# One transposition of the recurrence a slot later in another PSUM bank, and the attention statistics transposed as a whole tile, a slot later

## The chip, the cores and the metric

The kernel runs on one core of one Trainium2 chip. The metric is the device time of one execution in microseconds; "before" and "after" are compared by the median of several runs. A profile of one execution (a hardware trace) says which engine did what at which time.

The engines named here: TensorE (PE) multiplies matrices, and its weight loads are listed apart as PEld. VectorE (DVE) and ScalarE (ACT) do elementwise work, GpSimd (POOL) a little of it, and SyncE (SP) issues nearly all DMAs. Each engine carries out its own instructions in their order, and waits on semaphores for the others. SBUF is the on-chip memory of 128 partitions; PSUM is the memory that TensorE writes into, in banks of 128 x 512 float32.

## The reference

A trunk of two post-norm layers on x of 1024 positions by 1024 features, all in float32. Layer 0 mixes tokens by dilated attention, layer 1 by a gated linear recurrence (HGRN2). A squared-ReLU MLP with 4096 hidden features follows each.

```python
for i in range(DEPTH):                       # DEPTH = 2
    if i % 2 == 0: y = dilated_attention_mixer(x, attn_w_in, attn_w_out)
    else:          y = hgrn2_mixer(x, hgrn_w_in, hgrn_w_out, hgrn_norm_g, lbs[i])
    x = layer_norm(ALPHA * x + y)
    y = squared_relu_mlp(x, w_up, w_down)
    x = layer_norm(ALPHA * x + y)
```

Attention has three head groups (window 128, 512, 2048; dilation 1, 4, 16) with 16 heads of 64 features each. In every group a query looks at itself and 128 keys behind it in its residue class. The groups are mixed by a softmax over their log-sum-exps:

```python
m = max(s, -1); p = exp(s - m); l = sum(p, -1)
o = (p / l) @ v;  lse = m + log(l)
out = sum_g softmax_g(lse)[g] * o[g]
```

So m and l (the "statistics" below) of all three groups must come together before the outputs are mixed. The recurrence works in chunks of 64 positions, with 8 heads of 128 features; its output is normalised per head and goes through an output projection:

```python
a = where(causal, q_dec @ k_dec.T, 0);  o = a @ v + q_dec @ state
o = o * rsqrt(mean(o*o, -1) + RMS_EPS) * norm_g      # per head
y = o @ w_out
```

## The kernel before

**Stages.** Attention (0 to about 975 us of the span), its output projection with LayerNorm (to 1135), MLP 0 (to 1745), the recurrence (to 2105), its output projection (to 2230), MLP 1 (to the end). Each float32 product is made of three products of high and low parts; in the attention's and the MLPs' projections the 2 x 2 blocks are multiplied by a Strassen-like scheme of seven.

**Attention.** A unit is a pair of heads in one group: 8 pairs x 3 groups (in the order g = 2, 1, 0) = 24 units, and two consecutive ones form a step group gi. One step group has 21 products, each of 12 matmuls; `product(n)` is slot n. Behind each product the program issues the small work that a table put into that slot. For a step group the tables count from `base`, the slot 21 behind the group's first product: its units are worked off while the next group's products run. `OFFS` places six pieces of each unit (`qk`, `vtrans`, `ptr`, `pv`: scores, and the transpositions of v and of the probabilities, and the product with v), `ROPES` the rotary embedding, `STATS` the three steps of `combine_tr`, `MIX` the mixing of the groups (`combine`, `combine_mul`). Unit a=0 of the group has its pieces in slots 4, 6, 8, 10, 12 and 14, unit a=1 in 13, 15, 17, 19, 21 and 23. Within a slot, what was placed by an earlier group comes first, then unit 0's pieces and statistics, then unit 1's. The `in_order` block keeps TensorE and VectorE to the order of the program throughout this loop.

For each query block `qk` takes the (negated) maximum on VectorE (L511) and the exponentials with their sum on ScalarE (L514), and both leave one column in the unit's tile `stats`, 128 x 32: m and l, two heads, eight blocks. `combine_tr` then does three steps: it transposes that tile on TensorE (`mpt`, L564) into a bank of the tag `pt` and copies it out on ScalarE (`sr`, L566); writes it to DRAM (`mdram`, L569); and reads it back rearranged into `ml` (L575, L578). PSUM tags have fixed numbers of banks: `mm` 3, `s` 2, `pt` 2, `o` 1. All transpositions, and the broadcast `fb` of the mixing weights, take `pt`.

After the last step group, what is left of the tables (`done`) and the work of the last two units (`mine`) is put together in 22 lists, which the output projection works off between its own matmuls. There the order on TensorE is not written out. List 9 has unit b's `qk(4)`, list 10 unit a's last `ptr` and all three steps of its `combine_tr`, list 11 unit b's `qk(6)`.

**Recurrence.** For each of 8 heads there are six projections of 24 matmuls (L171 to L173), one per slot, and behind each the program issues one list of the head before: `trans` of v, both `amat`, `trans` of the keys; `kv(0)`; `omat(0)` and `kv(1)`; `omat(1)`; an empty list; `otr(0)` and `otr(1)`. `omat(j)` leaves half j normalised in `on` (VectorE, L1563), `otr(j)` transposes it in four pieces on TensorE (`opt`, L1571, into a `pt` bank), and ScalarE scales it into `oN` (L1572). For heads 0 to 4 the result goes to DRAM. Head 0 has one empty list in front. The lists of consecutive heads are merged index by index, so what a head has beyond six lists falls into the next head's first. The last head's lists are worked off by the output projection, evenly over its 56 steps of three matmuls.

Of the kernel before, what the change touches and what calls it, by code (L numbers as in the profile page):

```python
# [9 lines left out]
F32 = mybir.dt.float32  # L10
F32R = mybir.dt.float32r
U8 = mybir.dt.uint8
AF = mybir.ActivationFunctionType
# [3 lines left out]
P = 128  # L17
# [35 lines left out]
RESIDENT = 2  # L53
MIX = ((20, 21, 21, 24, 25, 30, 31, 32, 33, 33, 34, 35, 35, 36),
       (30, 31, 33, 34, 35, 37, 38, 39, 41, 41, 42, 42, 42, 43))
STATS = ((12, 13, 15), (21, 22, 24))
ROPES = ((-5, -3, -3, -1, 1, 2), (5, 7, 7, 9, 11, 11))
ROPES0 = ((-5, -2, -1, 2), (-4, 0, 1, 4))
OFFS = ((1, 3, 5, 7, 9, 11), (10, 12, 14, 16, 18, 20))
# [3 lines left out]
def trunk_kernel(  # L63
# [24 lines left out]
    nc = tc.nc  # L88
    cp = ctx.enter_context(tc.tile_pool(name="cp", bufs=1))
# [6 lines left out]
    def U(name, dt=F32):  # L96
        return up.tile([P, 1024], dt, name=name, tag="u")

    def bank(tag, name):
        return ps.tile([P, 512], F32, name=name, tag=tag, bufs={"mm": 3, "s": 2, "pt": 2, "o": 1}[tag])  # L100

    def small(shape, name, bufs=4, dt=F32):
        return sp.tile(shape, dt, name=name, tag=name, bufs=bufs)

    act = nc.scalar.activation
# [21 lines left out]
    ident = cp.tile([P, P], F32, name="ident")  # L127
# [194 lines left out]
    def attention(pre, hc):  # L322
# [120 lines left out]
        sel = cp.tile([P, NG * P], F32R, name="bsel")  # L443
        frow = U("frow", F32R)
        mdram = dp.tile([NPAIR, NG, 2, 2, S], F32, name="mdram")

        def constants():
            nc.sync.dma_start(cosT, cos_t)
            nc.sync.dma_start(sinT, sin_t)
            nc.sync.dma_start(mask, masks)  # L450
# [15 lines left out]
        def rope(e, g, nm):  # L466
            rot = U("rot")
            for b4 in range(4):
                o = (b4 ^ 1) * 32
                nc.sync.dma_start(rot[b4 * 32:b4 * 32 + 32, :], e[o:o + 32, :])  # L470
            qT = U(nm)
            nc.vector.tensor_mul(cls(qT, g), nat(e, g), nat(cosT, g))
            return qT, (lambda: nc.vector.tensor_mul(rot, rot, sinT),
                        lambda: nc.vector.tensor_add(cls(qT, g), cls(qT, g), nat(rot, g)))
# [84 lines left out]
                [lambda: pv(6), lambda: pv(7)],  # L559
            ]  # L560

        def combine_tr(pr, g, sS, ml):
            pt = bank("pt", "mpt")
            nc.tensor.transpose(pt[:32, 0:P], sS.rearrange("p w a b -> p (w a b)"), ident)  # L564
            sr = small([32, P], "sr", 2)
            act(sr, pt[:32, 0:P], AF.Copy)  # L566
            yield
            md = mdram[pr, g]
            nc.sync.dma_start(md.rearrange("w h (b q) -> (w h b) q", q=P), sr)  # L569
            yield  # L570

            d = DIL[g]
            for w in range(2):
                if d == 1:
                    nc.sync.dma_start(ml[:, w, 0, :], md[w].rearrange("h (i n) -> (h i) n", n=P))  # L575
                else:
                    for h in range(2):
                        nc.sync.dma_start(  # L578
                            ml[8 * h:8 * h + 8, w, g, :].rearrange("i (r n) -> i r n", r=d),
                            md[w, h].rearrange("(r i n) -> i r n", r=d, i=8))  # L580
            yield

        def combine(pr, ml):
            def cv(tl, g):
                d = DIL[g]
                return tl if d == 1 else tl.rearrange("p (r n) -> p n r", r=d)

            m = ml[:, 0]
            l = ml[:, 1]
            v = nc.vector  # L590
            mn = small([16, P], "mn", 1)
            v.tensor_tensor(nat(mn, 1), nat(m[:, 0], 1), cv(m[:, 1], 1), op=ALU.min)
            v.tensor_tensor(nat(mn, 2), nat(mn, 2), cv(m[:, 2], 2), op=ALU.min)
            for g in range(NG):
                v.tensor_sub(cv(m[:, g], g), nat(mn, g), cv(m[:, g], g))
            act(m, m, AF.Exp)
            yield
            v.tensor_mul(l, l, m)
            den = mn
            v.tensor_add(nat(den, 1), nat(l[:, 0], 1), cv(l[:, 1], 1))  # L600
            v.tensor_add(nat(den, 2), nat(den, 2), cv(l[:, 2], 2))
            yield
            v.reciprocal(den, den)
            for g in range(NG):
                v.tensor_mul(nat(l[:, g], g), cv(m[:, g], g), nat(den, g))

            fh = wp.tile([P, 512], F32R, name="fh", tag="p")[:16, :NG * P].rearrange("p (g t) -> p g t", t=P)
            fl = wp.tile([P, 512], F32R, name="fl", tag="pts")[:16, :NG * P].rearrange("p (g t) -> p g t", t=P)
            act(fh, l, AF.Copy)
            yield  # L610
            v.tensor_sub(fl, l, fh.bitcast(F32))
            yield
            for g in range(NG):
                for i, f in enumerate((fh, fl)):
                    r = 4 * g + 2 * i
                    nc.sync.dma_start(frow[r:r + 2, :].bitcast(F32).rearrange("h (i t) -> h i t", t=P),
                                      f[:, g, :].bitcast(F32))
            yield

        def combine_mul(pr, og, hb):  # L620

            c = slice(hb * 512, hb * 512 + 512)
            acc = og[0]
            for g in GORD:
                fb = bank("pt", "fb")
                nc.tensor.matmul(fb, sel[:, g * P:(g + 1) * P], frow[:, c], start=True, stop=True)
                nc.vector.tensor_mul(og[g][:, c], og[g][:, c], fb)
                yield
            nc.vector.tensor_add(og[2][:, c], og[2][:, c], og[1][:, c])
            nc.vector.tensor_add(acc[:, c], acc[:, c], og[2][:, c])  # L630
            yield
            if hb:
                if pr < SPILL[0]:
                    nc.sync.dma_start(ond[0, pr], acc)
                    oN.append(ond[0, pr])
                else:
                    oN.append(acc)
            yield
# [4 lines left out]
        def at(slot, f):  # L643
            fill.setdefault(slot, []).append(f)

        ep, acc, part = {}, {}, {}
        ml, ogs = {}, {}
# [58 lines left out]
        def unit_work(gi, a, base):  # L706

            pr, g = groups[gi][a]
            if pr not in ml:
                ml[pr] = small([16, 2, NG, P], "ml", 1)  # L710
                ogs[pr] = [None] * NG
            sS = small([P, 2, 2, 8], "stats", 3)

            adds = {}

            def rope_of(t):
                res[a, t], adds[t] = rope(ep.pop((gi, a, 0 if t == 1 else 1)), g, "qT" if t == 0 else "kT")

            def begin():
                ogs[pr][g] = U("og")  # L720
                p = pieces(pr, g, res.pop((a, 0)), res.pop((a, 1)), ep.pop((gi, 2, a)), ogs[pr][g], sS)
                for f in p[0]:
                    f()
                work.extend(p[1:])

            work = []
            later = [lambda: [f() for f in work.pop(0)] for _ in range(5)]
            trs = combine_tr(pr, g, sS, ml[pr])
            stats = [lambda: next(trs, None)] * 3
            mix = []  # L730
            if g == GORD[-1]:
                steps = combine(pr, ml[pr])
                mix = [lambda: next(steps, None)] * 5
                for hb in range(2):
                    muls = combine_mul(pr, ogs[pr], hb)
                    mix += [lambda muls=muls: next(muls, None)] * (4 + hb)
            return adds, rope_of, [begin] + later, stats, mix
# [23 lines left out]
        for n in range(len(seq)):  # L761
            gi, i, j = seq[n]
# [26 lines left out]
            if n % 21 == 14:  # L789
# [3 lines left out]
                for a in range(2):  # L793
                    adds, rope_of, core, stats, mix = work[a]
# [9 lines left out]
                    for k, f in enumerate(core):  # L804
                        at(base + UNIT0 + OFFS[a][k], f)
                    for k, f in zip(STATS[a], stats):
                        at(base + k, f)
# [677 lines left out]
    def hgrn(xs, late, consts, pre, gw):  # L1485
# [8 lines left out]
        def head_pieces(hd, kd, kd2, qd, vT, dec, oNt):  # L1494
# [71 lines left out]

            def otr(j):
                on = st.pop(("on", j))
                pt = bank("pt", "opt")
                for i in range(4):  # L1570
                    nc.tensor.transpose(pt[:, i * P:(i + 1) * P], on[:, i * P:(i + 1) * P], ident)  # L1571
                act(oNt[:, j * 512:(j + 1) * 512], pt, AF.Identity, scale=gT[:, hd:hd + 1])  # L1572
                if hd < SPILL[1] and j == 1:
                    nc.sync.dma_start(ond[1, hd], oNt)
# [4 lines left out]
                [lambda: omat(0), lambda: kv(1)],  # L1579
                [lambda: omat(1)],  # L1580
                [],
                [lambda: otr(0), lambda: otr(1)],
            ]

        oN = []
# [3 lines left out]
        for hd in range(8):  # L1589
# [8 lines left out]
            for t, h in slots:  # L1598
# [7 lines left out]
                o = proj(loaded[bi], xs[h])  # L1606
# [8 lines left out]
                if both and t == 1:  # L1615
# [14 lines left out]
                    b = a1  # L1630
# [9 lines left out]
                if both and t == 0:  # L1640
                    q = e[0]
# [27 lines left out]
    pr = Out(w_attn_out, "a", 0)  # L1669
# [7 lines left out]
    pr = Out(w_hgrn_out, "h", 1)  # L1677
# [81 lines left out]
```

## Time and profile before

| | us |
|---|---|
| median of 3 runs | 2845.02 (2842.76 to 2846.17) |
| profiled execution | 2844.54 |
| its span | 2842.8 |
| TensorE busy | 2772.0 (98%) |
| TensorE weight loads | 2229.9 (78%) |
| VectorE busy | 2068.6 (73%) |
| ScalarE busy | 1449.2 (51%) |
| GpSimd busy | 122.7 (4%) |

The span goes from the first to the last instruction of the trace, and the execution's own time has 1.7 us around it. A row of a timeline gives start, length, engine, line, operation, what it writes <- reads, shape and count, and in brackets the engine's idle time before it with what ended it. In shapes such as 128*32 stand the rows and columns of TensorE's array that a matmul uses. Consecutive like instructions are merged into one row; its length is then from the first start to the last end. Ends of matmuls are modelled, and a matmul's end lies behind the start of the next one in an undisturbed stream. A row of waits gives who waited for whom, us in total, times and the longest. A row of windows gives the stretch and its length, the busy time and number of instructions of PE, PEld, DVE, ACT and POOL, and then the granted clock of TensorE, the mean busy share of the DMA engines, and GB/s. Engine names with a q (SPq) are the sequencers that issue DMAs.

### The profile page before, as it was taken

To read this page: it belongs to the slowest core of one execution; us is meant where nothing else is said; L and a number is where in the kernel's file an instruction comes from. 1 tells how busy PE (TensorE), PEld (TensorE's weight loads), DVE (VectorE), ACT (ScalarE), POOL (GpSimd) and SP (SyncE) were. 2 spreads that over 40 slices of the span, in tenths; PEclk is the share of its full clock that TensorE was granted. 3 is DMA by queue.
4 is the path that set the end of the run, shared out by engine and by line. 5 is a ranking of instruction groups with operands and counts; after the bars stand their busy time and mean duration, and the time that the engine had idled before them with its cause. 6 is when DMAs were issued, how large, how long until landed. Compare 5 with 4: busy or idle time off the path is not lost. (4 is left out here: it accounts for less than half of the span.)

```text
span 2842.8 us, 40144 instructions
## 1 busy us (share of the span) xinstructions
PE 2772.0 (98%) x14280; PEld 2229.9 (78%) x14280; DVE 2068.6 (73%) x3830; ACT 1449.2 (51%) x3105; POOL 122.7 (4%) x67
## 2 busy tenths in 40 slices
PE   8999999999999989999999999999999999999998
PEld 6777777777777767888878887787787788878887
DVE  7768777777777767786686876565667787678677
ACT  5555555555555555544454434555553545454433
POOL 0000000000000003100000011111102200000000
PEclk9999999999999999999999999999999999999999
DMA  7766665766667523464494752101132455475654
GB/s 288 252 200 195 185 206 172 216 198 206 193 194 219 166 87 133 145 226 156 158 320 126 263 177 90 38 31 60 55 117 81 149 204 174 159 271 189 222 175 132
DMA packets 204936, 485.27 MB, mean 171 GB/s; under 512 B 29376, under 2 KB 43712, under 8 KB 204736
## 3 DMA queue, kind: packets, MB, share of 16 engines
q1 hardware_dynamic: 204736, 482.72, 51.5%
q8 instruction: 112, 1.84, 0.3%
q14 instruction: 88, 0.72, 0.1%
HBM read 362.82 MB, written 94.24 MB: 161 GB/s over the span
## 5 line engine op out<-in xcount | busy, mean ns | idle before, releaser
L666 PE MATMUL pmm<-xh,H 128*128 128x512 f32 x1008 | 407.6, 404 | 13.0 <-ACT H L432 8.9
L668 PE MATMUL pmm<-xh,H 128*128 128x512 f32 x1008 | 395.7, 393 | 0.1
L667 PE MATMUL pmm<-xl,H 128*128 128x512 f32 x1008 | 395.6, 392 | 0.0
L666 PEld LDWEIGHTS pmm<-xh,H 128*128 128x128 f32 x1008 | 190.9, 189 | 53.3 <-ACT H L432 8.9
L668 PEld LDWEIGHTS pmm<-xh,H 128*128 128x128 f32 x1008 | 190.2, 189 | 42.3 <-DVE H L440 0.8
L667 PEld LDWEIGHTS pmm<-xl,H 128*128 128x128 f32 x1008 | 191.0, 189 | 36.6
L514 ACT ACTIVATE p<-p,stats 128x128 f32<-128x128 f32 (+1 forms) x384 | 168.3, 441 | 93.6 <-DVE stats L511 92.2
L1260 PE MATMUL pdy<-dT,dS 128*128 128x512 f32 x512 | 199.2, 389 | 0.0
L1263 PE MATMUL pdy<-dT,dS 128*128 128x512 f32 x512 | 199.2, 389 | 0.0
L1264 PE MATMUL pdy<-dT,dS 128*128 128x512 f32 x512 | 199.2, 389 | 0.0
L511 DVE CUSTOM_DVE_ANT_0 p<-s,mask 128x128 f32<-128x128 f32 (+1 forms) x384 | 113.3, 348 | 67.7 <-PE s L500 58.4
L137 ACT ACTIVATE dS<-dr 128x512 fp32r<-128x512 f32 x192 | 119.5, 622 | 73.2 <-PE pdy L1264 36.6
L171 PE MATMUL pmm<-f0nh,wh 128*128 128x512 f32 x384 | 153.2, 399 | 0.0
L173 PE MATMUL pmm<-f0nh,wl 128*128 128x512 f32 x384 | 149.9, 390 | 1.6 <-DVE wl L138 1.6
L172 PE MATMUL pmm<-f0nl,wh 128*128 128x512 f32 x384 | 149.7, 390 | 0.0
L138 DVE TENSOR_TENSOR dS<-dr,dS 128x512 fp32r<-128x512 f32 x192 | 136.2, 710 | 15.8 <-ACT dS L137 13.9
L214 POOL TENSOR_TENSOR z<-z,bB 128x1024 f32<-128x1024 f32 x24 | 58.5, 2442 | 1680.8 <-ACT z L213 1676.7
L527 ACT ACTIVATE pts<-ppt 128x256 f32<-128x256 f32 (+1 forms) x192 | 85.4, 474 | 62.0 <-PE ppt L524 59.8
L137 ACT ACTIVATE dT<-hold 128x512 fp32r<-128x512 f32 x128 | 80.0, 625 | 69.9 <-DVE hold L1239 28.8
L1073 ACT ACTIVATE H<-wc 128x512 fp32r<-128x512 f32 x128 | 77.2, 625 | 73.5 <-DVE wc L1066 44.0
L1263 PEld LDWEIGHTS pdy<-dT,dS 128*128 128x128 f32 x512 | 96.1, 188 | 20.1
L1260 PEld LDWEIGHTS pdy<-dT,dS 128*128 128x128 f32 x512 | 96.1, 188 | 19.8
(395 smaller groups left out, 6950.3 us busy)
## 6 DMA issues: line engine op xcount, KB each, us to landing
xh<-xtd SPq DMA_DIRECT2D x110, 512.0 KB
xl<-xtd SPq DMA_DIRECT2D x110, 512.0 KB
dr<-hd SPq DMA_DIRECT2D x192, 256.0 KB
dr<-in_w_down_dram SPq DMA_DIRECT2D x128, 256.0 KB
rot<-e SPq DMA_DIRECT2D x192, 128.0 KB
wa<-in_w_up_dram SPq DMA_DIRECT2D x48, 512.0 KB
wb<-in_w_attn_dram SPq DMA_DIRECT2D x36, 512.0 KB
wa<-in_w_attn_dram SPq DMA_DIRECT2D x33, 512.0 KB
```

The source lines that it names most:

```text
L137: act(hi, raw, AF.Copy)
L138: nc.vector.tensor_sub(lo, raw, hi.bitcast(F32))
L171: nc.tensor.matmul(o, wh[:, k], xs.h(k), start=k == 0, stop=False)
L172: nc.tensor.matmul(o, wh[:, k], xs.l(k), start=False, stop=False)
L173: nc.tensor.matmul(o, wl[:, k], xs.h(k), start=False, stop=k == NK - 1)
L514: act(p[:, h, :n], p[:, h, :n], AF.Exp, bias=sS[:, 0, h, b:b + 1], scale=-1.0, accum_out=sS[:, 1, h, b:b + 1])
L666: nc.tensor.matmul(o, wh, hi[k // 2][:, c], start=begin and k == 0, stop=False, skip_group_check=True)
L667: nc.tensor.matmul(o, wh, lo[k // 2][:, c], start=False, stop=False, skip_group_check=True)
L668: nc.tensor.matmul(o, wl, hi[k // 2][:, c], start=False, stop=end and k == 3, skip_group_check=True)
L1260: nc.tensor.matmul(o[q], h, T_[:, L], start=begin, stop=False, skip_group_check=True)
L1263: nc.tensor.matmul(o[q], h, T_[:, R], start=False, stop=False, skip_group_check=True)
L1264: nc.tensor.matmul(o[q], l, T_[:, L], start=False, stop=end, skip_group_check=True)
```

## The change

In the recurrence `otr(1)` gets a list of its own behind `otr(0)`'s, a slot later, and its transpositions go into the one `o` bank instead of a `pt` bank. A head has seven lists then, and `otr(1)` falls into the first list of the head after, ahead of that head's `trans`. In the output projection the last head's lists are spread as seven over the same 56 steps.

In attention the `stats` tiles of the units become four slices of 32 columns of one tile `allS` of 128 x 128, zeroed once; unit number 2 gi + a takes slice (2 gi + a) mod 4. `combine_tr` transposes the whole tile and copies and stores only its own 32 rows. All three of its steps are placed one slot later.

```diff
-STATS = ((12, 13, 15), (21, 22, 24))
+STATS = ((13, 14, 16), (22, 23, 25))
...
+        allS = cp.tile([P, P], F32, name="stats")
+        nc.gpsimd.memset(allS, 0.0)
...
-        def combine_tr(pr, g, sS, ml):
+        def combine_tr(pr, g, slot, ml):
             pt = bank("pt", "mpt")
-            nc.tensor.transpose(pt[:32, 0:P], sS.rearrange("p w a b -> p (w a b)"), ident)
-            sr = small([32, P], "sr", 2)
-            act(sr, pt[:32, 0:P], AF.Copy)
+            nc.tensor.transpose(pt[:, 0:P], allS, ident)
+            q = slice(slot * 32, slot * 32 + 32)
+            sr = small([P, P], "sr", 2)
+            act(sr[q], pt[q, 0:P], AF.Copy)
             yield
             md = mdram[pr, g]
-            nc.sync.dma_start(md.rearrange("w h (b q) -> (w h b) q", q=P), sr)
+            nc.sync.dma_start(md.rearrange("w h (b q) -> (w h b) q", q=P), sr[q])
...
-            sS = small([P, 2, 2, 8], "stats", 3)
+            slot = (2 * gi + a) % 4
+            sS = allS[:, slot * 32:slot * 32 + 32].rearrange("p (w a b) -> p w a b", w=2, a=2)
...
-            trs = combine_tr(pr, g, sS, ml[pr])
+            trs = combine_tr(pr, g, slot, ml[pr])
...
             def otr(j):
                 on = st.pop(("on", j))
-                pt = bank("pt", "opt")
+                pt = bank("o" if j else "pt", "opt")
...
-                [lambda: otr(0), lambda: otr(1)],
+                [lambda: otr(0)],
+                [lambda: otr(1)],
```

## The prediction

> **What bounds the kernel now.** I read the page's busy shares first, then TensorE's waits over the whole run, longest first, then the timelines around the two waits that the change touches.
>
> ```profile
> span 2842.8 us, 40144 instructions
> PE 2772.0 (98%) x14280; PEld 2229.9 (78%) x14280; DVE 2068.6 (73%) x3830; ACT 1449.2 (51%) x3105; POOL 122.7 (4%) x67
> ```
>
> TensorE sets the end: it is busy 98% of the span and the next engine 73%. Its idle time is 2842.8 - 2772.0 = 70.8 us, so what it stops waiting for comes off the end, unless another wait takes its place.
>
> ```profile
> PE opt L1571 <- DVE on L1563: 7.3, 5, 1.6
> PE pmm L183 <- ACT aoh L137: 4.9, 3, 3.6
> ...
> PE mpt L564 <- ACT pts L527: 3.5, 13, 0.3
> ...
> PE mpt L564 <- DVE og L627: 1.4, 3, 0.5
> ```
>
> Each row gives who waited, for whom, us in total, times, longest. The change addresses rows one, three and four: opt (the mixer's second transposition) idles 7.3 us in 5 waits, mpt (the statistics) 3.5 + 1.4 = 4.9 us in 16. Row two belongs to the seam between attention and its output projection.
>
> **The mixer's wait.** On TensorE (start, length, line, shape, count, idle before it):
>
> ```profile
> 1877.54 0.60 PE L1571 MATMUL opt<-ident,on 128*128 128x128 f32 x4
> 1879.69 0.66 PE L1571 MATMUL opt<-ident,on 128*128 128x128 f32 x4 [1.55 <-DVE on L1563]
> 1880.10 0.48 PE L171 MATMUL pmm<-f0nh,wh 128*128 128x512 f32 x1
> ```
>
> and, from the same view of VectorE:
>
> ```profile
> 1878.95 0.68 DVE L1563 TENSOR_TENSOR on<-ho,rms 128x512 f32<-128x512 f32 x1
> ```
>
> The first four transpositions are otr(0), the second four otr(1). otr(1) waits for its input, which VectorE ends at 1878.95 + 0.68 = 1879.63. What a wait costs is more than the idle it shows, because a matmul is counted busy until its modelled end while the next one normally starts before that. Undisturbed, eight of them run so (in the out-projection behind the mixer):
>
> ```profile
> 2152.30 1.03 PE L1571 MATMUL opt<-ident,on 128*128 128x128 f32 x8
> 2153.10 0.49 PE L183 MATMUL pmm<-woh,hoh 128*128 128x512 f32 x1
> ```
>
> 0.80 us from the first to the next matmul, 0.10 each. With the wait it is 1880.10 - 1877.54 = 2.56. The wait costs 1.76, its idle 1.55 and 0.21 more. Five waits: 7.3 + 5 x 0.21 = 8.3 us.
>
> After the change otr(1) goes behind the next head's first projection. That is 24 matmuls of 512 columns, 0.23 apart (the rows at 287.20 and 287.43 below), so 5.5 us after otr(0)'s end at 1877.54 + 0.44: near 1883.5, when its input has been ready for 3.9 us. No wait is left. Its four transpositions cost the same 0.4 there as here. It stands first in a list that issues 8 transpositions, 16 matmuls and 8 transpositions; I look at what they wait for:
>
> ```profile
> 1885.68 1.03 PE L1503 MATMUL hpt<-ident,vTh 128*128 128x128 f32 x8
> 1886.55 1.95 PE L1511 MATMUL as<-qe,ls 128*128 128x128 f32 x16
> 1888.33 1.04 PE L1503 MATMUL hpt<-ident,ze 128*128 128x128 f32 x8
> ```
>
> ```profile
> 1885.87 0.60 ACT L1607 ACTIVATE ze<-pmm 128x512 f32<-128x512 f32 x1 [3.85 <-PE pmm L173]
> 1886.37 1.08 ACT L1504 ACTIVATE vn<-hpt 128x512 f32<-128x512 f32 x2
> ```
>
> The second eight need the two pt banks that ScalarE empties by 1886.37 + 1.08 = 1887.45, 0.88 ahead of 1888.33. In front of them ScalarE now also empties otr(1)'s bank, 0.5 us (as from 1885.87 to 1886.37), while TensorE comes 0.4 later: 0.8 us of slack stays. Without that cover it would cost 0.1 a head. The bank is the o bank, of which there is one; omat(0) takes it two lists on, some 17 us later, so I put this at nothing. Mixer: **-8.3**, bounds -7.3 (idle alone) and -8.8 (8.3 with 0.1 per wait for the slower first transposition behind it).
>
> **The statistics' wait.** Slot 12 of an undisturbed group:
>
> ```profile
> 364.78 0.49 PE L524 MATMUL ppt<-ident,p 128*128 128x128 f32 x3
> 365.53 0.28 PE L564 MATMUL mpt<-ident,stats 128*32 128x128 f32 x1 [0.26 <-ACT pts L527]
> 365.57 0.49 PE L666 MATMUL pmm<-xh,H 128*128 128x512 f32 x1
> ```
>
> Three transpositions of 0.11 end their turn at 365.11; mpt starts at 365.53, since both pt banks are in use by ptr(6) and ptr(7) just ahead of it. So 0.42 is lost where the idle shown is 0.26, again 0.16 more. Sixteen waits: 4.9 + 16 x 0.16 = 7.5 us. One slot later nothing stands ahead of mpt but a product (and in some groups one fb), and both banks are free. For a=1 (slot 22) no work of the list follows. For a=0 (slot 13) the other unit's qk(0) and vtrans come behind it, and vtrans wants both pt banks:
>
> ```profile
> 287.20 0.39 PE L668 MATMUL pmm<-xh,H 128*128 128x512 f32 x1
> 287.43 0.39 PE L626 MATMUL fb<-frow,bsel 128*128 128x512 f32 x1
> ...
> 288.60 1.09 PE L488 MATMUL vpt<-ident,vT 128*128 128x128 f32 x8
> ```
>
> ```profile
> 287.62 0.60 ACT L697 ACTIVATE e<-pmm 128x512 f32<-128x512 f32 x1 [2.50 <-PE pmm L668]
> 289.03 0.40 ACT L514 ACTIVATE p<-p,stats 128x128 f32<-128x128 f32 x1 [0.81 <-DVE stats L511]
> ```
>
> mpt starts near 287.7; ScalarE is free from 288.2 to 289.0, and the copy of mpt (128 columns, against 512 in the eviction's 0.60) ends by 288.8, ahead of vtrans' second bank at 288.7 + 0.44. Bound: if it loses here what it gained in slot 12, the 11 groups give back 11 x 0.42 = 4.6.
>
> The transposition itself is now 128 columns of weights instead of 32:
>
> ```profile
> L1571 PEld LDWEIGHTS opt<-ident,on x64: 138/140/143, 1838.7 to 2153.0; 128*128 128x128 f32 x64
> L564 PEld LDWEIGHTS mpt<-ident,stats x24: 93/94/103, 120.2 to 1038.9; 128*32 128x32 f32 x24
> ```
>
> 140 - 94 = 46 ns, 24 x 46 = 1.1 us if all of it shows, nothing if the 0.23 us matmul ahead hides it. Since loads of 140 ns run at one transposition per 0.10 us, I take nothing. The Trainium skill, "TensorE: Matmul & The Clock Gate", section "LDWEIGHTS (loading the stationary operand)", speaks against the whole tile: it has a load grow with its columns, columns / 1.2 ns, an estimated 80 ns more each, 1.9 us in all, by which the forecast would be 2831.4. The rows have the sign and 46 ns.
>
> Besides: one memset at the start (GpSimd is 4% busy), the same ScalarE copies and as many DMAs. The 32-column slices are disjoint, so the only new order is that mpt reads the whole tile: it must wait for every earlier statistic of either unit. In the loop the last ones ahead of an mpt are three slots old, and the next come behind it. Only in the tail do the units alternate: list 10 holds unit a's mpt, list 9 unit b's qk(4).
>
> ```profile
> 1029.52 0.27 PE L564 MATMUL mpt<-ident,stats 128*32 128x128 f32 x1
> ```
>
> ```profile
> 1030.57 0.20 ACT L514 ACTIVATION_READ_ACCUMULATOR p<-p,stats 128x1 f32 x1
> ```
>
> ```profile
> 1031.61 0.34 SPq L569 DMA_DIRECT2D mdram<-sr  x1
> ...
> 1040.04 0.33 SPq L569 DMA_DIRECT2D mdram<-sr  x1
> ```
>
> If those are b's last exponentials of qk(4), mpt waits from 1029.52 to 1030.77: 0 to 1.3 us, once. SP's queue behind 1031.61 shifts as much, but has 5 us until unit b's own write. I take 0.6 **later**.
>
> **The DMAs moved.** SP issues in order and waits at the write of the statistics; weights are queued behind it:
>
> ```profile
> SPq L569 <- ACT sr L566: 149.5, 21, 13.7
> ```
>
> ```profile
> 204.07 0.33 SPq L569 DMA_DIRECT2D mdram<-sr  x1
> ...
> 207.76 0.38 SPq L405 DMA_DIRECT2D wa<-in_w_attn_dram  x1
> ```
>
> ```profile
> 214.00:216.00 2.00, 2.00 (x18) 1.45 (x17) 1.04 (x4) 0.22 (x2) 0.00 (x0) 1.00 0.05 18
> ```
>
> ```profile
> 218.01 1.67 ACT L432 ACTIVATE H<-wa 128x512 fp32r<-128x512 f32 x3
> ```
>
> The weights issued at 207.76 have landed by about 214.1 (after 214 the DMA share, last but one, is 0.05 of 2 us) and are the last of the three read from 218.01 on, from 218.01 + 2/3 x 1.67 = 219.1: 5.0 us in hand. A slot is 12 matmuls of 0.23, 2.8 us, 3.1 where an fb or mpt itself adds to it. 1.9 us stays: nothing, but this is the thinnest cover of the change.
>
> **Sum** against the profiled execution, 2844.54 us (span 2842.8 and 1.7 around it; the three runs have a median of 2845.02): -8.3 - 7.5 + 0.6 = -15.2, so 2829.3; I say **2829.5**.
>
> **The rivals.**
> (1) Only the idle shown comes back: 7.3 + 4.9 - 0.6 = 11.6, 2832.9. For it: busy time is all the page counts; against it: the starts above.
> (2) mpt's wait goes along to slot 13 or 22, as a bank wait of vtrans or of fb: the mixer alone, 2844.5 - 8.3 + 0.6 = 2836.8. For it: the two pt banks serve all the transpositions and fb.
> (3) otr(1) stays where it was or waits as long in its new place (the mixer has no written order on TensorE): attention alone, 2844.5 - 7.5 + 0.6 = 2837.6. Against it: the projection is earlier in program order and its weights are there.
> (4) Slower: SP. If the statistics' write keeps the weights behind it back by more than 5.0 us, instead of 3.1, ScalarE, in order, stands still for `wa` in each of 11 groups, and the evictions behind it hold TensorE's banks. Every us beyond 5.0 costs 11; from 2 us (write and reads both falling behind the loads of the next slot) it is 22, more than all the gain: 2829.3 + 22 = 2851. For it: the 149.5 us that SP already waits there; against it: 1.9 us in hand, and weights are split five slots ahead of their use.
> (5) A clock effect, which moves the range alone. TensorE ran at half its clock (last but two column of a window's row: the granted clock) after two longer idle times, the seam's and one early in the run, and at full clock through the mixer's waits:
>
> ```profile
> 118.50 0.33 PE L539 MATMUL o<-pts,vn 128*64 128x128 f32 x2 [2.09 <-ACT og L550]
> ```
>
> ```profile
> 120.00:122.00 2.00, 1.95 (x6) 1.47 (x6) 0.00 (x0) 1.88 (x5) 0.00 (x0) 0.50 0.07 23
> ...
> 1050.00:1052.00 2.00, 2.00 (x6) 1.58 (x5) 2.00 (x6) 0.14 (x1) 0.00 (x0) 0.50 0.00 0
> ...
> 1879.69:1925.10 45.41, 44.00 (x277) 36.49 (x277) 27.45 (x42) 24.05 (x34) 4.79 (x2) 1.00 0.14 47
> ```
>
> So the waits of 1.55 that go give no clock back. A seam that is longer or shorter by the 1.3 us above can gain or lose a window of 2 us at half clock, 1 us each; two for the low end, one for the high. The Trainium skill, same page, section "Why this matters for your kernels", warns of idle gaps over about 3 us; the seam's 3.6 agrees with it, the 2.09 does not.
>
> **How the numbers follow.** Forecast 0.60; (1) 0.12; (2) 0.09; (3) 0.05; (4) 0.06; both gains mostly lost in waits I don't see, near 2842, 0.08. Low end: 8.8 + 8.0 (with 0.5 for statistics that wait too shortly to be listed) + 2 of clock = 18.8, so 2825.5. High end: past (2) and (3), 2838. 0.2% is 5.7 us, about what a measurement of this kernel can tell from no change: faster than 2839.3 are the forecast and (1) to (3), 0.86; within it 0.08; slower 0.06.
>
> **What would show it.** In the waits of the changed kernel the opt row is gone and both mpt rows are gone in the loop; otr's four and four stand a projection apart; no new row above 1 us on vpt, hpt, or on a pmm for `H`. In the tail one mpt wait on `p`. Wrong would be: SP's wait at the statistics grown and ScalarE waiting for `wa`; a row of 0.4 us x 11 on vpt; the opt row still there; or a span that falls by idle only.

## The result, and the profile after

The changed kernel takes 2828.6 us (median of 4 runs, 2826.27 to 2829.86), the kernel before beside it on the same chip 2843.89 us (4 runs, 2842.29 to 2846.17). That is 15.3 us less. The ratio on record is 0.9941, with a 95% interval of 0.9929 to 0.9953; the quotient of these two medians, 0.9946, lies within it. The profiled execution took 2828.98 us.

The page's busy shares of the changed kernel:

```profile
span 2827.2 us, 40131 instructions
...
PE 2766.7 (98%) x14280; PEld 2229.3 (79%) x14280; DVE 2069.0 (73%) x3830; ACT 1450.8 (51%) x3105; POOL 122.9 (4%) x68
```

The span fell by 15.6 us. TensorE's idle time fell from 70.8 to 2827.2 - 2766.7 = 60.5, by 10.3; the other 5.3 came out of its *busy* time, with the same 14280 matmuls. A reader who counts idle time alone sees two thirds of the gain. TensorE's waits, longest first:

```profile
PE pmm L669 <- ACT H L432: 9.6, 1, 9.6
...
PE ppt L526 <- DVE og L630: 3.0, 6, 0.8
...
PE ppt L526 <- ACT pts L529: 2.8, 6, 0.5
PE fb L629 <- DMA frow<-fh: 2.5, 1, 2.5
```

The opt row (7.3 us) and both mpt rows (4.9 us) are gone from the list. No vpt or hpt row has taken their place, and in the loop only one wait of 0.2 us for `H`. The `H` row shown is the start-up's one wait (8.9 before), and the `ppt` rows stand in the profile before with the same numbers, on the two banks that mpt now takes a slot later. The wait that has grown most is fb's; before it was

```profile
PE fb L626 <- DMA frow<-fh: 0.8, 1, 0.8
```

The mixer's transpositions on TensorE:

```profile
1869.94 0.60 PE L1575 MATMUL opt<-ident,on 128*128 128x128 f32 x4
1870.30 0.48 PE L171 MATMUL pmm<-f0nh,wh 128*128 128x512 f32 x1
...
1875.86 0.60 PE L1575 MATMUL opt<-ident,on 128*128 128x128 f32 x4
1876.30 1.04 PE L1507 MATMUL hpt<-ident,vTh 128*128 128x128 f32 x8
```

otr(0) and otr(1) stand 5.9 us apart, with a projection between them, and neither has a bracket with idle time. Before, the pair held TensorE for 2.56 us; now each four takes 0.36 to 0.44. The same engine in slot 13 of an attention group, where the moved mpt meets qk(0) and vtrans:

```profile
366.03 0.27 PE L566 MATMUL mpt<-ident,stats 128*128 128x128 f32 x1
366.23 0.93 PE L502 MATMUL s<-kT,qT 64*128 64x128 f32 x8
367.09 1.09 PE L490 MATMUL vpt<-ident,vT 128*128 128x128 f32 x8
367.94 0.48 PE L669 MATMUL pmm<-xh,H 128*128 128x512 f32 x1
```

vtrans takes 367.94 - 367.09 = 0.85 us, as in every one of these slots before. Of the 11 in the changed kernel ten take 0.85 and the last, at 940.6, takes 1.08; no wait is listed for it.

To place the gain, compare one kind of matmul in each stage, first and last start. Before, first the attention's products from the second group to the start of the last, then the recurrence's projections:

```profile
L667 PE MATMUL pmm<-xl,H x843: 387/389/628, 73.7 to 892.6; 128*128 128x512 f32 x169
...
L171 PE MATMUL pmm<-f0nh,wh x384: 387/389/501, 1750.0 to 2104.2; 128*128 128x512 f32 x192
```

and the same two rows of the changed kernel:

```profile
L670 PE MATMUL pmm<-xl,H x843: 387/389/628, 74.0 to 885.9; 128*128 128x512 f32 x169
...
L171 PE MATMUL pmm<-f0nh,wh x384: 387/389/501, 1742.1 to 2088.2; 128*128 128x512 f32 x192
```

The attention loop went from 818.9 to 811.9, **-7.0 us**; the recurrence from 354.2 to 346.1, **-8.1 us**. What is left of the 15.6, -0.5, is small things of both signs: from the last product to MLP 0's first matmul it took 0.8 us more, where fb waits, and a stretch at half clock near 1744 us is missing in this execution (last section).

### The profile page after: what moved, and what is told of

The parts are those of the page before. It is cut to its first block, busy times and chain, and to the rows that moved or that the text cites. A ratio compares the mean times of both kernels' runs of the same rounds, so it can differ in the third digit from the quotient of the medians.

```text
span 2827.2 us, 40131 instructions
## 1 busy us (share of the span) xinstructions
PE 2766.7 (98%) x14280; PEld 2229.3 (79%) x14280; DVE 2069.0 (73%) x3830; ACT 1450.8 (51%) x3105; POOL 122.9 (4%) x68
## 4 chain that ended last, share of the span: by engine, by line
PE 90%; DVE 5%; ACT 2%; DMA 1%; issue 1%; POOL 0%; SPq 0%; DVEq 0%; POOLq 0%; ACTq 0%
PE pmm L669 8%; PE pmm L671 8%; PE pmm L670 8%; PE pup L1118 7%; PE pup L1116 7%; PE pup L1117 7%; PE pdy L1268 4%; PE pdy L1264 4%; PE pdy L1267 4%; PE s L502 3%; PE pdx L1267 3%; PE pmm L171 3%; PE pdx L1268 3%; PE pmm L173 3%; PE pdx L1264 3%; PE pmm L172 3%
```

## The experiments

**Each half alone.** The mixer's half on the kernel before:

```diff
-                pt = bank("pt", "opt")
+                pt = bank("o" if j else "pt", "opt")
...
-                [lambda: otr(0), lambda: otr(1)],
+                [lambda: otr(0)],
+                [lambda: otr(1)],
```

> The kernel before with the recurrence's part alone (otr(1) a slot later and in the o bank). The theory of the prediction: each of five waits costs its idle and 0.2 us more, so 8.3 us come off, ratio 0.9971. If only the idle shown counts: 7.3 us, 0.9974. If the parts are not independent (the attention part frees the mixer's): well under 8 us. On the trace: no wait of opt, and head 2 to head 7 of the recurrence shorter by 8 to 9 us.

Measured: 2835.83 us against 2844.15, ratio 0.9969 (0.9957 to 0.9981), 8.3 us less. The projections' row:

```profile
L171 PE MATMUL pmm<-f0nh,wh x384: 387/389/501, 1749.7 to 2095.3; 128*128 128x512 f32 x192
```

345.6 us instead of 354.2, -8.6. The attention's half, on the kernel before:

```diff
-STATS = ((12, 13, 15), (21, 22, 24))
+STATS = ((13, 14, 16), (22, 23, 25))
...
-            nc.tensor.transpose(pt[:32, 0:P], sS.rearrange("p w a b -> p (w a b)"), ident)
+            nc.tensor.transpose(pt[:, 0:P], allS, ident)
```

> The kernel before with the attention part alone (one tile of statistics, transposed whole, a slot later). Theory: 7.5 us off and 0.6 to 0.9 back in the tail, so 6.6 to 6.9 off, ratio 0.9976. If only idle counts: 4.9 - 0.8 = 4.1, 0.9986. On the trace the loop of products is shorter by 7 us (theory) or 5 us (idle alone).

Measured: 2837.8 us, ratio 0.9976 (0.9966 to 0.9986), 6.4 us less. The product of the two ratios is 0.9945, the change's own 0.9941: the two gains add, as far as intervals of 0.001 either way can tell.

**In the mixer: the slot or the bank?** The new list without the new bank (otr(1) stays in `pt`):

```diff
-                [lambda: otr(0), lambda: otr(1)],
+                [lambda: otr(0)],
+                [lambda: otr(1)],
```

> The kernel before with otr(1) a slot later, but in a pt bank as before. Theory A, the slot does it and the bank is free of charge either way: same as the mixer part alone, 8.3 us off, within 1 us. Theory B, the bank matters: otr(1) takes the pt bank that the next head's second group of v transpositions wants 0.9 us later, while ScalarE first empties the projection (0.5) and then this bank (0.5): 0.3 to 0.5 us of wait on hpt in each of 7 heads, 2 to 3.5 us less gain, so 5 to 6 off. I expect B.

and the new bank without the new list:

```diff
-                pt = bank("pt", "opt")
+                pt = bank("o" if j else "pt", "opt")
```

> The kernel before with otr(1) in the o bank, but in the same list as otr(0). Its input is as late as before, so both theories expect no change (within 1 us), with the five waits of opt on VectorE still there, 7.3 us. If the waits were in truth for the pt bank, they go here and 8 us come off.

Measured: the list alone 2837.04 us, 0.9973 (0.9962 to 0.9983); the bank alone 2844.6 us, 1.0002 (0.9993 to 1.0011). The bank by itself does nothing, and its wait row says why: VectorE's `on` is late, not the bank.

```profile
PE opt L1571 <- DVE on L1563: 7.2, 5, 1.6
```

Whether the bank adds to the list can't be told from the two times (the intervals of 0.9969 and 0.9973 overlap), but the traces show it. The recurrence with the list alone:

```profile
L171 PE MATMUL pmm<-f0nh,wh x384: 389/389/501, 1746.0 to 2093.8; 128*128 128x512 f32 x192
```

is 347.8 us, 2.2 more than with the bank. TensorE behind otr(1), first with list and bank:

```profile
1882.94 0.60 PE L1571 MATMUL opt<-ident,on 128*128 128x128 f32 x4
1883.37 1.04 PE L1503 MATMUL hpt<-ident,vTh 128*128 128x128 f32 x8
...
1886.83 0.48 PE L171 MATMUL pmm<-f0nh,wh 128*128 128x512 f32 x1
```

then with the list alone:

```profile
1880.66 0.60 PE L1571 MATMUL opt<-ident,on 128*128 128x128 f32 x4
1881.09 0.60 PE L1503 MATMUL hpt<-ident,vTh 128*128 128x128 f32 x4
1881.53 0.61 PE L1511 MATMUL as<-qe,ls 128*128 128x128 f32 x4
1882.08 0.66 PE L1503 MATMUL hpt<-ident,vTh 128*128 128x128 f32 x4
...
1884.71 0.48 PE L171 MATMUL pmm<-f0nh,wh 128*128 128x512 f32 x1
```

Without the second bank the eight hpt no longer run through: the second four come after four of the `as` matmuls, and the list takes 4.05 us instead of 3.89. As I read it, their bank still holds otr(1)'s result. No opt or hpt row shows these 0.16 us among the waits; in five heads they make 0.8 us. Another 0.9 us are lost once, where otr(1) of head 0 stands ahead of `kv(0)`, which takes two `pt` banks (last section). The other 0.5 us lie ahead of the first otr, and I don't know their cause. So the list carries the gain, and the `o` bank keeps 1.7 us of it. That fits the second theory, at somewhat less than its 2 to 3.5 us.

**In attention: the slot or the whole tile?** The slot alone, each unit with its own 32-column tile:

```diff
-STATS = ((12, 13, 15), (21, 22, 24))
+STATS = ((13, 14, 16), (22, 23, 25))
```

> The kernel before with the statistics' transposition and its two followers one slot later, each unit keeping its own 32-column tile. Theory (the slot frees the two pt banks, the shape does nothing): the mpt rows leave TensorE's waits, about -7.5 us, a ratio near 0.9974, the same as with the whole tile. Rival (the whole tile is needed for the gain, or costs some of it): a ratio at least 0.001 away from that of the statistics part alone, which was 0.9976; by the 46 ns of the longer weight load the 32-column form would be 1.1 us faster, 0.9972.

and the whole tile alone, in the old slots:

```diff
-            nc.tensor.transpose(pt[:32, 0:P], sS.rearrange("p w a b -> p (w a b)"), ident)
+            nc.tensor.transpose(pt[:, 0:P], allS, ident)
```

> The kernel before with the statistics in one tile, transposed as a whole, in the old slots. Theory (the shape is free and gains nothing): both mpt rows stay, 16 or 17 waits of 4.9 us, ratio 1.000, at most 1.0004 if the 46 ns of the weight load show (1.1 us) in the waits. Rival (the whole tile carries part of the gain): the mpt rows shrink and the ratio falls below 0.999.

Measured: the slot alone 2837.65 us, 0.9975 (0.9966 to 0.9985), the same as the whole half (0.9976); the tile alone 2845.25 us, 1.0004 (0.9995 to 1.0013). With the tile alone the waits stay:

```profile
PE mpt L566 <- ACT pts L529: 3.7, 14, 0.3
PE mpt L566 <- DVE og L630: 1.4, 3, 0.5
```

So the gain is the slot's; the whole tile neither gives nor takes what these runs can tell (about 2.6 us). The run with the tile alone also shows the end of the loop, where I had forecast a new wait for mpt. TensorE in list 10 of this kernel, and its last mpt:

```profile
1030.72 0.70 PE L502 MATMUL s<-kT,qT 64*128 64x256 f32 x2
...
1032.16 0.70 PE L502 MATMUL s<-kT,qT 64*128 64x256 f32 x2
1032.78 0.33 PE L566 MATMUL mpt<-ident,stats 128*128 128x128 f32 x1
...
1040.21 0.27 PE L566 MATMUL mpt<-ident,stats 128*128 128x128 f32 x1
```

Before, mpt stood 0.21 us ahead of the first of these pairs (1029.52, the pair at 1029.73). Now it stands behind the second, 2.06 us after the first, and no bracket shows idle time. In this stretch the order on TensorE is not written out; as I read it, the program was laid out with mpt after what it must wait for. The first pair came 0.99 us later than before, the last mpt 1.20 (1039.01 before); the 0.21 between is the place of the first mpt itself, which now lies between them. At this place the tail's wait costs nothing.

**The cover behind SP's write.** Here the forecast was thinnest: weights queue behind the write of the statistics. SP's issues in the changed kernel:

```profile
206.96 0.33 SPq L572 DMA_DIRECT2D mdram<-sr  x1
...
210.28 0.38 SPq L405 DMA_DIRECT2D wa<-in_w_attn_dram  x1
```

and ScalarE's use of them:

```profile
217.61 1.67 ACT L432 ACTIVATE H<-wa 128x512 fp32r<-128x512 f32 x3
```

The semaphore that tells of the weights issued at 210.28 has its last update at 217.00; they are read from 217.61 + 2/3 x 1.67 = 218.7: 1.7 us in hand. In the group around 700 us nothing is in hand. There the third weights are issued at 701.94, the semaphore is complete at 710.13, and ScalarE has waited for them:

```profile
710.15 0.63 ACT L432 ACTIVATE H<-wa 128x512 fp32r<-128x512 f32 x1 [2.04 <-DMA wa<-in_w_attn_dram]
```

The loop of the kernel before has no such wait. TensorE has no wait for `H` in this group, so these 2.04 us cost nothing. To use the cover up, I moved the statistics another slot:

```diff
-STATS = ((13, 14, 16), (22, 23, 25))
+STATS = ((14, 15, 17), (23, 24, 26))
```

> The changed kernel with the statistics one more slot later (two in all). It tests the cover that my forecast called the thinnest. SP's write is 2.8 us later again, the tightest weights had 2.15 us left, so two or three of the 11 groups' loads come up to 1 us after their use would start. Theory (ScalarE waits about 1 us for wa in a few groups, and the split's five slots ahead of use swallow it): no loss, ratio 0.994 as the change, ScalarE's waits for wa appear. Rival 4 of the forecast (late weights hold TensorE's banks): 11 us per us beyond the cover, 3 to 11 us slower than the change, ratio 0.995 to 0.998, with pmm waits for H in the loop.

Measured: 2826.86 us, 0.9938 (0.9925 to 0.9951), as the change. But the run did not test what it was made for. SP's issues in the same group:

```profile
203.69 0.33 SPq L405 DMA_DIRECT2D wa<-in_w_attn_dram  x1
210.08 0.33 SPq L572 DMA_DIRECT2D mdram<-sr  x1
```

A slot further, the write falls behind the weights in program order, and they are no longer held back. A cover in an issue queue is not a distance in time alone; it depends on which side of it the transfer stands. So I moved the weights themselves, to k = 1, 2 and 3 slots later:

```diff
-            load_w(n + LOADW)
+            load_w(n + LOADW - (k if n >= 21 else 0))
```

> The changed kernel with every load of attention weights issued one slot (2.9 us) later from the second group on. In the changed kernel the third weights of groups 3, 6 and 9 land 2.2 us before ScalarE reads them, those of the other groups 5.5 us or more; so three loads land about 0.7 us late, 2 us in all. Theory (ScalarE's five slots between split and use hide it): no loss, ratio within 0.0005 of the change's 0.9941. Rival 4 of the forecast: 2 us slower, 0.9948.

> The same, two slots (5.8 us) later. Three loads land about 3.6 us late and two about 0.3, at most 13 us in all. Rival 4 (what ScalarE waits, TensorE waits): up to 11 us slower than the change, ratio near 0.998, with pmm waits for the evictions behind. Theory (the split is five slots, 14 us, ahead of its use, and an eviction has some slack of its own): still no loss, 0.994, though ScalarE's waits for wa show.

> The same, three slots (8.7 us) later: a load is issued in the slot of its own split. By the margins of the changed kernel all groups from the third on land late, by 2 to 6.5 us, some 35 us of ScalarE's waits in all. Rival 4: up to 30 us slower than the change, ratio above 1.00. Theory: ScalarE's stalls now hold evictions; the loss is that part which exceeds the eviction's slack, 5 to 15 us, ratio 0.996 to 0.999.

Measured: k = 1 2828.67 us, 0.9948 (0.9934 to 0.9963); k = 2 2829.24 us, 0.9949 (0.9934 to 0.9964); k = 3 2840.23 us, 0.9986 (0.9977 to 0.9996). The first two intervals hold the change's 0.9941, the third does not. The attention's products with k = 2:

```profile
L670 PE MATMUL pmm<-xl,H x843: 387/389/628, 73.7 to 885.7; 128*128 128x512 f32 x169
```

and with k = 3:

```profile
L670 PE MATMUL pmm<-xl,H x843: 387/389/632, 73.6 to 898.2; 128*128 128x512 f32 x169
```

812.0 us against the change's 811.9 with two slots (812.3 with one), and 824.6 with three. With one and two slots loads were late, and ScalarE waited for them. Its waits in the loop with k = 1:

```profile
ACT H L432 <- DMA wa<-in_w_attn_dram: 4.3, 5, 1.5
```

With k = 2 they are 3.8 us in 4, and in the changed kernel the one wait of 2.0. So loads that came up to 2 us late for ScalarE cost no time that these traces show, as the theory had it, though with k = 1 there are five of them and not three. With k = 2 far less was late than the 13 us that I expected: the third weights of group 3, issued at 217.44, are read at 224.63, one stretch of work later than before. The order on ScalarE is not written out, and the program had moved the read too. With k = 3 the late loads cost time, by another way than I had named. ScalarE has no wait for `wa` in the loop; VectorE, which forms the combined weights, waits for `wb`:

```profile
DVE wc L423 <- DMA wb<-in_w_attn_dram: 27.0, 14, 4.3
```

and behind it TensorE for `H`:

```profile
769.86 0.50 PE L671 MATMUL pmm<-xh,H 128*128 128x512 f32 x1 [2.06 <-DVE H L440]
```

VectorE's 27.0 us of waits came with 12.7 us lost on TensorE, about half. Some 1.7 of them belong to one more stretch at half clock near 101 us.

**The waits that remain.** The ppt rows that stand in both profiles looked to me of the same kind: `ptr` takes a `pt` bank that an fb, placed ahead of it in the slot by the mixing of an earlier group, still holds. On the changed kernel I moved the mixing steps so that no fb stands ahead of a ptr in one slot:

```diff
-MIX = ((20, 21, 21, 24, 25, 30, 31, 32, 33, 33, 34, 35, 35, 36),
-       (30, 31, 33, 34, 35, 37, 38, 39, 41, 41, 42, 42, 42, 43))
+MIX = ((20, 21, 21, 24, 25, 30, 32, 35, 36, 37, 39, 41, 41, 42),
+       (30, 31, 33, 34, 35, 37, 39, 41, 41, 43, 44, 45, 45, 46))
```

> The changed kernel with the mixing steps that own an fb product placed so that none stands in one slot ahead of a ptr, which shares its pt banks. What waits remain in the loop on these banks are ppt for og (3.0 us in 6) and for pts (2.8 us in 6). Theory (a bank wait goes when the neighbours in the list no longer share the tag; it costs its idle and 0.16 us hidden): both ppt rows go, 5.8 + 12 x 0.16 = 7.7 us less than the changed kernel, near 2820 us, ratio about 0.9915. Rival (the mixing moved later holds the tiles it reads, or the last steps spill into the next group): one wait replaced by another on og, fs or H, ratio 0.994 or more.

The same edit on the kernel before:

> The kernel before with the mixing steps moved as in the version with fb apart, nothing else. Theory (every wait is a neighbour in its own list, so the gains add): the ppt rows go, 6 to 8 us less, ratio 0.9973 to 0.9978, mpt and opt rows as before. Rival (the ppt waits only move behind mpt, which still stands in front): ratio above 0.9985.

Measured: on the change 2821.26 us, 0.9919 (0.9905 to 0.9933); on the kernel before 2836.05 us, 0.9972 (0.9961 to 0.9982). The attention's products with both:

```profile
L670 PE MATMUL pmm<-xl,H x843: 387/389/628, 74.3 to 879.6; 128*128 128x512 f32 x169
```

805.3 us, 6.6 less than the change's 811.9 and 13.6 less than before. Both ppt rows are gone from the waits of both kernels; with the edit alone, the longer mpt row (3.5 us in 13) and the opt row stay as they were, but the mpt row for `og` (1.4 us in 3) goes too, which I had not expected.

So neighbours that share a bank's tag can be parted one pair at a time, and the gains nearly add: 15.3 and 8.4 us alone, 23.1 together. The 1.4 us of that row can be gained only once. The kernel with both is the fastest here: 2821.26 us, though its interval touches that of the change, and the 6.6 us come from the trace of one execution each.

## Why the prediction was right

I had said 2829.5 us and a sum of -15.2 from the profiled execution; it measured 2828.6, and -15.6 in the profile. The two large terms came out by the mechanism that I had named; the small ones, tail and clock, by luck. (The low end of the range is by its own terms 2844.5 - 18.8 = 2825.7, not 2825.5.)

**The mixer, -8.3.** Right: 8.3 us by the medians of the mixer's half alone, 8.6 in its trace. The upper bound, 8.8, and the lower, idle alone 7.3, hold it. The step that made the difference was to count what a wait costs between starts, 1.76 us and not the 1.55 shown: the five pairs held TensorE for 12.30 us before, 8.3 more than five undisturbed ones of 0.80. The cover named there, ScalarE's 0.8 us ahead of the second eight hpt, held. What I put at nothing, the `o` bank, is nothing for the one that takes it, but it is worth 1.7 us against staying in `pt`: my step about hpt looked only at the keys' transpositions, and with one tag the first eight and `kv(0)` would have been hit.

**The statistics, -7.5.** Right in kind, a little large: 7.0 us in the loop of the change, 6.4 by the medians of its half alone, 6.7 by the slot's (each known to about 2.8 us). From execution to execution the loop differs by about 2 us, but the two kinds stay apart: with the mixing left as it was, it takes 818.3 to 820.5 us in the five profiles with the old slots, and 810.2 to 812.3 in the six with later ones and no load three slots late. The bound of 4.6 us given back in slot 13 did not come: vtrans takes its 0.85 us there in ten of 11 groups, and 0.2 more in one.

**Idle and hidden.** The forecast had 12.2 us of idle and 5 x 0.21 + 16 x 0.16 = 3.6 us that the page counts as busy. The page after has 10.3 less idle (fb's longer wait takes 1.7 back) and 5.3 less busy. The half-clock stretch that is missing (last section) accounts for 1.7 of the busy time, which leaves 3.6. That it fits so exactly is luck, in one pair of profiles; rival 1, idle alone, falls by the 8.3 to 8.6 us of the mixer's half, whose idle was 7.3, and by the loop's 7.0, where mpt's idle was 4.6.

**The weight load, nothing.** The transposition's load is 45 ns longer, as forecast:

```profile
L566 PEld LDWEIGHTS mpt<-ident,stats x24: 138/139/142, 124.0 to 1032.2; 128*128 128x128 f32 x24
```

With the 32-column tiles in the new slots the kernel takes 2837.65 us, with the whole tile 2837.8. The Trainium skill, "TensorE: Matmul & The Clock Gate", section "LDWEIGHTS (loading the stationary operand)", gave an estimated 80 ns more; the rows have 45. The 1.1 us that these would make are less than the two times can tell (about 2.8 us).

**The tail, +0.6: the step that failed.** I had mpt wait for unit b's exponentials. The whole tile does make mpt depend on them, but mpt changed its place among the matmuls instead, and its cost there is nothing (the run with the tile alone). Some 0.8 us were lost near there all the same, where fb waits 2.5 us for its DMA instead of 0.8. The run with the bank alone, whose attention is the kernel before's, waited as long at that place:

```profile
PE fb L626 <- DMA frow<-fh: 2.4, 1, 2.4
```

So that wait differs from run to run without the change. In the 14 profiles the stretch from the last product to MLP 0's first matmul takes 144.1 to 146.2 us (144.1 before, 145.0 after), and the 0.8 can't be put down to the change. The size was right by luck.

**SP's cover, 1.9 us left.** Right in group 3, 1.7 us; wrong in the group around 700 us, where the load came 2.0 us late. The forecast had read one group, and the landing from the DMA share: by its semaphore that load landed at 214.70 before, so 4.4 us were in hand and not 5.0. That late loads are hidden there is what saved the step, and rival 4's price, 11 us for each us beyond the cover, is wrong: 2.0 us in one group, and with k = 1 up to 1.5 us in five, cost nothing. With three slots late loads do slow the loop, but the engine that waits first is VectorE for `wb`, not ScalarE for `wa`, and TensorE lost about half of what VectorE waited, not all of it. That the reserve is the five slots between a split and its use is argued from the code, and no run shows it by itself.

**Rivals 2 and 3** fall with the rows: mpt's wait did not go along to slot 13 or 22, and otr(1) did not wait in its new place.

**The clock** took 1.7 us from the profiled execution (last section), within the 2 us that the range allowed, but not at the seam that I had named. The trace before has a stretch at half clock near 1744 us that the forecast did not count, and it is this one that is missing after.

## What to carry to other kernels

Where TensorE waits in a slot for a late input, or for a PSUM bank that a neighbour in the same slot still holds, part the two by a slot of other work: here that alone made the gains, while the shape of the tile and the other bank by themselves made none. Price a wait on a busy TensorE by the starts on both sides of it, and not by its idle time, which hides 0.16 to 0.21 us of each. And before you trust a thin cover in an issue queue, look at every group, not one, and move the transfer itself to see where the time breaks; its neighbours in program order decide as much as its distance, and a load that is late for its reader need not be late for the kernel.

## What the runs showed of the hardware that I had not expected

**The same idle time is not always followed by the half clock.** TensorE's wait between MLP 0 and the recurrence, before:

```profile
1742.48 0.63 PE L223 MATMUL lnpt<-ident,z 128*128 128x128 f32 x4 [2.14 <-DVE f0nl L234]
```

```profile
1742.00:1744.00 2.00, 1.52 (x9) 1.31 (x10) 1.44 (x5) 0.66 (x2) 0.60 (x1) 0.95 0.78 258
1744.00:1746.00 2.00, 2.00 (x6) 1.60 (x5) 1.17 (x3) 0.80 (x2) 0.00 (x0) 0.50 0.96 297
1746.00:1748.00 2.00, 2.00 (x8) 1.56 (x7) 0.35 (x1) 1.06 (x1) 0.00 (x0) 0.70 1.03 422
```

and after, where 1737 to 1739 is the same place:

```profile
1736.19 0.63 PE L223 MATMUL lnpt<-ident,z 128*128 128x128 f32 x4 [2.14 <-DVE f0nl L234]
```

```profile
1737.00:1739.00 2.00, 2.00 (x11) 1.61 (x10) 1.43 (x4) 1.32 (x4) 0.00 (x0) 1.00 1.00 301
```

The same 2.14 us, and the clock is 0.50 in one and 1.00 in the other. All 14 profiles have this wait of 2.1 us; five of them have the half-clock stretch behind it, nine do not, with and without the edits. By the three rows it costs 2 x (0.05 + 0.50 + 0.30) = 1.7 us, as much as one of the waits that the change takes away; one profile against one profile can be wrong by that.

**The order of matmuls on 64 rows decides whether they run in pairs.** The recurrence's state products (`kv(0)`), with list and bank:

```profile
1848.69 1.16 PE L1523 MATMUL kvps<-vn,k2n 64*128 64x128 f32 x16
```

and in the run with the list alone:

```profile
1845.53 2.05 PE L1523 MATMUL kvps<-vn,k2n 64*128 64x128 f32 x16
```

In the first run they start in pairs, two within 7 ns and most pairs 0.11 us apart; in the second they start one by one, 0.11 us apart, and take 0.9 us more. The program has them in another order there: the weight loads that wait for a semaphore are the first and second of the sixteen in the first run, the first and ninth in the second, so one bank's eight stand ahead of the other's. `kv(0)` writes two `pt` banks in turn, and in this one list otr(1), in a `pt` bank itself, stands just ahead of it. That this is why the order changed is argued from the code; the 97 other such groups of the 14 profiles, none with otr(1) in `pt` just ahead, take 1.16 us.
